# Three modulation products of the second layer leave the first layer's mixers

## The chip, the core and the metric

The kernel runs on one core of a Trainium2 chip. The metric is the time in microseconds (us) that the device needs for one execution; the time of the kernel before is the median of three runs. The core has a matrix engine (PE, with its weight loads as PEld), a vector engine (DVE), a scalar engine (ACT), a general engine (POOL) and a queue engine (SP) that does nothing here but issue transfers. ACT can issue transfers too. Each engine runs its own instructions in the order in which they stand in the program; semaphores hold an instruction back until what it needs is there.

## The reference, cut to what matters

Two layers of a network run over 1024 latent tokens and 256 context tokens of width 1024, all in f32:

```
for l in range(2):
    need_ctx = l < 1
    mod_l = split(silu(c)     @ ada_w[l] + ada_b[l], 6)     # latent rows
    mod_c = split(silu(c_ctx) @ ada_w[l] + ada_b[l], 6)     # context rows
    h  = rmsnorm(x, norm1_w[l])   * (1 + mod_l[1]) + mod_l[0]
    hc = rmsnorm(ctx, norm1_w[l]) * (1 + mod_c[1]) + mod_c[0]
    y, yc = four mixers (RG-LRU, HGRN2, SSD, MLA attention) of h @ w_in[l], hc @ w_in[l]
    x = x + mod_l[2] * (y @ w_out[l])
    h = rmsnorm(x, norm2_w[l]) * (1 + mod_l[4]) + mod_l[3]
    x = x + mod_l[5] * expert_choice_ffn(h, ...)            # 16 experts
    if need_ctx: the same for ctx with yc and mod_c
```

`ada_w[l]` is 1024 x 6144. Its six blocks of 1024 columns are needed at different times: blocks 0 and 1 by the first norm of a layer, block 2 behind the mixers, blocks 3 to 5 by the second norm and the experts. They depend on `c` and `c_ctx` alone, so each can be computed at any time ahead of its use.

## The kernel before

A layer runs as a set of threads (Python generators): `norm1` (first norm and the transposes of its 10 tiles of 128 tokens), the projections by `w_in` (`v` among them: 24 matmuls 128x256 a tile, evicted by ACT and written to memory from ACT's queue), the four mixers, `prep` and `mla` (attention: each prepared tile of queries and keys goes through memory and is read back by L1343), `lw` (loads of `w_out`), `wout` (the output projection, second norm and the router's logits), `route` (the choice of tokens for each expert), `woutc` and `routec` (the same for the context) and `exp` (the 16 experts). `Model.weave` steps the threads in turn by a table of priorities (`ORDER`; the lower the number, the earlier a thread is stepped) and by an account of when each engine comes free, and so fixes the order of the instructions on each engine. A thread stops at `wait(...)` until the named marks are in `self.done`, and at `room(n, "W")` until n tiles of the kind are free. Weights lie in tiles of 512 KB, tag `W`, of which there are 7.

`ada(l, i)` computes modulation blocks 2i and 2i+1 of layer l. It takes 8 steps; in each, two transfers on SP's queue bring 512 KB each of `ada_w` into `W` tiles (L405), and four f32 matmuls of 32x512 (`sT`, the activated `c` and `c_ctx`, against them) add to one accumulator, in four column groups of the array. In the trace one such matmul is two records, so a step is 8. Behind the 8 steps DVE adds the bias and ACT's queue writes the two rows to memory (L419). Product (0, 0) has its own thread at the kernel's start. The other five, (0, 1), (0, 2), (1, 0), (1, 1) and (1, 2), stand one behind another in the thread `ada` of layer 0, whose priority 20 puts its steps where the mixers leave room.

All transfers of SP's and ACT's queues share eight semaphores in turn, and a transfer that gets a semaphore waits until the one that had it before has landed. So a long run of transfers on one queue can hold up the other queue's.

Of the kernel before, what the change touches and what calls it, by code (L numbers as in the profile page):

```python
# [29 lines left out]
ORDER = [  # L30
    dict(derived=0.5, ada0=-2, ada=20, norm=-3, eproj=6.624, lru0=6.01, lru1=8.078, gate0=8.48, gate1=7.01, ssd=4.653,
         z=8.49, g=7, v=1.85, hgrn0=6.614, hgrn1=0.99, group0=1.91, group1=4.161, hout0=4.306, hout1=1.492, chunk=3.42,
# [8 lines left out]
    dict(derived=0.5, ada0=-2, ada=20, norm=-3, eproj=1, lru0=6.01, lru1=8.078, gate0=3.4, gate1=7.01, ssd=3.43, z=6.95,  # L41
         g=7, v=0.079, hgrn0=6.614, hgrn1=6.757, group0=1.91, group1=3.41, hout0=6.767, hout1=3.44, chunk=6.713, prep=1.5,
# [123 lines left out]
class Model:  # L166
# [210 lines left out]

    def ada(self, l, i, first=False):

# [15 lines left out]
        for k in range(8):  # L395
            if first:
                ws = [W[k // 2][:, k % 2, 0:1024], W[k // 2][:, k % 2, 1024:2048]]
                yield 2.5
            else:
                yield from self.room(2, "W")  # L400
                ws = []
                for hf in range(2):
                    w = self.t("W", [128, 1024])
                    c0 = 2048 * i + 1024 * hf
                    nc.sync.dma_start(w, wk[k][:, c0:c0 + 1024])  # L405
                    ws.append(w)
                yield 5.0
# [10 lines left out]
        for s in range(0 if first else 2):  # L418
            nc.scalar.dma_start(self.mod[l, s, 2048 * i:2048 * i + 2048].rearrange("(g n) -> g n", g=4),  # L419
                                mr.rearrange("(g r) n -> r g n", r=32)[s])  # L420
        if i == 0:
            self.done.add(f"mod{l}")
# [1097 lines left out]
    def wout(self, l, s, base, h2d, logits):  # L1520

        nc, a = self.nc, self.a
        c0, nt = (0, 2) if s else (2, 8)
        yield from self.wait(f"w{l}.0", *([f"woutc{l}.1"] if l == 0 and not s else []))
        yield from self.room(4)
# [526 lines left out]
    def layer(self, l):  # L2052
        need = l == 0
        self.yT = self.d([1024, NT])
        if l == 0:
            self.spawn(l, "derived", self.derived())
            self.spawn(l, "ada0", self.ada(0, 0, True))
            self.spawn(l, "ada", chain(self.wait("n0.9"), *[self.ada(*x) for x in ((0, 1), (0, 2), (1, 0), (1, 1), (1, 2))]))
        self.left[l] = 18
# [76 lines left out]
```

## Time and profile before

| | us |
|---|---|
| median of three runs | 2833.26 (2833.19 to 2836.4) |
| the profiled execution, its own time | 2837.1 |
| its span in the trace | 2835.3 |
| PE busy | 2421.0 (85%) |
| DVE busy | 1830.6 (65%) |
| ACT busy | 1183.7 (42%) |
| POOL busy | 908.6 (32%) |

The profile's times count from the start of the span. Layer 0 takes the first 1578 us (mixers up to some 920, output projection to 1088, routing to 1131, experts to 1572), layer 1 the rest. Busy shares are means over stages with different limits, so that what counts is the stage from which work is taken, and the stages to which it goes: in layer 0 the attention's start and what follows (611 to 735), the routing (1088 to 1131), and in layer 1 the first norm and the projections (1578 to 1710).

### The profile page before, as it was taken

The numbers are of one execution on the slowest core, as the hardware profiler recorded it, in microseconds if no ns is written. First come the engines' busy times: TensorE is split into PE (matmuls) and PEld (weight loads), VectorE is DVE, ScalarE is ACT, GpSimd is POOL, SyncE is SP. The second block draws the span as 40 slices with busy tenths as digits, with TensorE's granted clock in tenths as the row PEclk, the third lists the DMA queues.
The fourth block names the chain that finished last, engine by engine and source line by source line (L and its number), as shares of the span: only waits on it lengthen the run. The fifth ranks groups of instructions, "written<-read, shape, count | busy, mean of one in ns | idle before, by whom it ended". The sixth has DMA issues, their size and how long they took to land. (4 is left out here: it accounts for less than half of the span.)

```text
span 2835.3 us, 49820 instructions
## 1 busy us (share of the span) xinstructions
PE 2421.0 (85%) x19212; PEld 1850.4 (65%) x19212; DVE 1830.6 (65%) x3606; ACT 1183.7 (42%) x2010; POOL 908.6 (32%) x930
## 2 busy tenths in 40 slices
PE   5879999988898794889899599889968988669998
PEld 3758888544555572767677587779745556447786
DVE  5345476566786546676677746672787764578886
ACT  3345223234344222555455352422352342246675
POOL 3112232242531113233343522421353311324443
PEclk8889999999999896999999799989988999879999
DMA  6222135468212434688788511132331023559997
GB/s 250 63 67 65 58 92 184 134 218 288 82 51 97 158 116 136 235 263 282 264 280 283 160 49 42 55 98 80 115 113 49 23 95 131 199 187 377 376 366 244
DMA packets 243436, 455.40 MB, mean 161 GB/s; under 512 B 25688, under 2 KB 155096, under 8 KB 242176
## 3 DMA queue, kind: packets, MB, share of 16 engines
q1 hardware_dynamic: 190176, 365.75, 37.1%
q0 software_dynamic: 12096, 37.75, 5.6%
q10 hardware_dynamic: 40928, 48.72, 4.9%
q8 instruction: 151, 2.47, 0.4%
q14 instruction: 85, 0.70, 0.1%
HBM read 377.55 MB, written 74.60 MB: 159 GB/s over the span
## 5 line engine op out<-in xcount | busy, mean ns | idle before, releaser
L162 PE MATMUL ps<-A,W 128*128 128x512 f32 (+3 forms) x4160 | 972.2, 381 | 34.4 <-ACT W L162 31.5
L162 PEld LDWEIGHTS ps<-A,W 128*128 128x128 f32 x4160 | 742.4, 196 | 180.1 <-ACT W L162 35.3
L162 DVE TENSOR_TENSOR A<-C,A 128x1024 fp32r<-128x1024 f32 x310 | 406.8, 1342 | 129.8 <-ACT A L162 123.9
L162 ACT ACTIVATE M<-ps 128x512 f32<-128x512 f32 (+6 forms) x576 | 262.4, 468 | 533.1 <-PE ps L162 448.8
L162 ACT ACTIVATE A<-C 128x1024 fp32r<-128x1024 f32 x384 | 394.6, 1059 | 180.0 <-DMA C<-in_moe_w_down_dram 76.6
L162 POOL TENSOR_TENSOR A<-C,A 128x1024 fp32r<-128x1024 f32 x74 | 206.2, 2789 | 319.6 <-ACT A L162 303.8
L162 PE MATMUL ps<-W,A 128*128 128x256 f32 x1344 | 191.7, 299 | 6.6 <-DVE A L162 6.3
L162 PE MATMUL ps<-A,M 128*128 128x512 f32 x768 | 182.9, 393 | 2.1 <-ACT M L162 1.4
L162 PEld LDWEIGHTS ps<-W,A 128*128 128x128 f32 x1344 | 176.4, 202 | 9.4 <-DVE A L162 7.0
L162 POOL TENSOR_TENSOR C<-C,M 128x512 f32<-128x512 f32 x76 | 110.1, 1459 | 190.4 <-ACT M L162 129.4
L162 PEld LDWEIGHTS ps<-A,M 128*128 128x128 f32 x768 | 142.4, 188 | 36.4 <-DVE M L162 3.0
L162 PE MATMUL ps<-cf,M 128*128 128x128 f32 (+3 forms) x416 | 75.0, 309 | 98.8 <-DVE M L162 63.9
L162 DVE TENSOR_TENSOR C<-C,M 128x512 f32<-128x512 f32 (+2 forms) x196 | 128.8, 669 | 40.7 <-ACT M L162 39.3
L162 PE MATMUL ps<-C,A 128*32 128x128 f32 (+1 forms) x2528 | 145.3, 285 | 0.0
L162 PEld LDWEIGHTS ps<-C,A 128*32 128x32 f32 (+1 forms) x2528 | 132.9, 125 | 11.3 <-issue 6.4
L162 PE MATMUL ps<-A 96*128 96x512 f32 (+3 forms) x368 | 132.3, 415 | 9.3 <-ACT A L162 4.0
L162 PEld LDWEIGHTS ps<-cf,M 128*128 128x128 f32 (+2 forms) x416 | 55.7, 157 | 128.7 <-issue 43.6
L162 PE MATMUL ps<-M,M 128*128 128x64 f32 (+4 forms) x720 | 90.4, 284 | 56.4 <-DVE M L162 46.1
L162 PE MATMUL ps<-A,C 128*128 128x512 f32 x352 | 134.0, 411 | 1.5 <-DVE C L162 1.4
L162 ACT ACTIVATE W<-ps 128x512 fp32r<-128x512 f32 (+2 forms) x156 | 65.9, 476 | 163.1 <-PE ps L162 162.7
L162 ACT ACTIVATE C<-ps 128x512 f32<-128x512 f32 (+4 forms) x116 | 53.8, 469 | 183.1 <-PE ps L162 170.0
L162 POOL TENSOR_TENSOR W<-W,C 128x512 f32<-128x512 f32 x33 | 49.7, 1524 | 249.4 <-DVE W L162 184.1
(244 smaller groups left out, 3838.0 us busy)
## 6 DMA issues: line engine op xcount, KB each, us to landing
C<-in_moe_w_gate_dram SPq DMA_DIRECT2D x128, 512.0 KB
C<-in_moe_w_up_dram SPq DMA_DIRECT2D x128, 512.0 KB
C<-in_moe_w_down_dram SPq DMA_DIRECT2D x128, 512.0 KB
W<-in_ada_w_dram SPq DMA_DIRECT2D x80, 512.0 KB
W<-in_w_in_dram SPq DMA_DIRECT2D x40, 512.0 KB
C<-dr SPq DMA_DIRECT2D x29, 512.0 KB
dr<-M ACTq DMA_DIRECT2D x114, 128.0 KB
M<-dr SPq DMA_DIRECT2D x46, 256.0 KB
```

Source lines behind the costliest of these rows:

```text
L162: return f(*args, **kw)
```

## The change

Product (1, 0), which the first norm of layer 1 needs, gets a thread of its own, `ada1`, with priority 32. It starts when tile 7 of layer 0's `wout` is done, that is in the routing, with its 16 loads on SP's queue. Products (1, 1) and (1, 2) move into layer 1, as its thread `ada` with priority 20; their 32 loads are issued on ACT's queue (`later=True`). `wout` now waits for the marks of its layer's products 1 and 2 as well. (0, 1) and (0, 2) stay where they were. The number of matmuls is the same.

```diff
-    dict(derived=0.5, ada0=-2, ada=20, norm=-3, eproj=6.624, ...
+    dict(derived=0.5, ada0=-2, ada=20, ada1=32, norm=-3, eproj=6.624, ...
...
-    def ada(self, l, i, first=False):
+    def ada(self, l, i, first=False, later=False):
...
-                    nc.sync.dma_start(w, wk[k][:, c0:c0 + 1024])
+                    (nc.scalar if later else nc.sync).dma_start(w, wk[k][:, c0:c0 + 1024])
...
+        self.done.add(f"ada{l}.{i}")
         if i == 0:
             self.done.add(f"mod{l}")
...
-        yield from self.wait(f"w{l}.0", *([f"woutc{l}.1"] if l == 0 and not s else []))
+        yield from self.wait(f"ada{l}.1", f"ada{l}.2", f"w{l}.0", *([f"woutc{l}.1"] if l == 0 and not s else []))
...
-            self.spawn(l, "ada", chain(self.wait("n0.9"), *[self.ada(*x) for x in ((0, 1), (0, 2), (1, 0), (1, 1), (1, 2))]))
+            self.spawn(l, "ada", chain(self.wait("n0.9"), *[self.ada(*x) for x in ((0, 1), (0, 2))]))
+            self.spawn(l, "ada1", chain(self.wait("wout0.7"), self.ada(1, 0)))
+        else:
+            self.spawn(l, "ada", chain(*[self.ada(1, i, later=True) for i in (1, 2)]))
```

Three places show what stands in an engine's row. In the rows, `W` tiles from `in_ada_w_dram` and matmuls with `sT` are the products'; `DMA M<-dr ... 128x384` is a query or key tile read back (L1343, in the kernel after the change L1344). The line numbers after the change are one higher from L420 on.

SP's queue in layer 0, where the attention reads its tiles back, before:

```order
L1343 DMA M_10192<-dr_8413 128x384
L384 DMA M_10210<-in_ada_b_dram 32x512 x4
L405 DMA W_10216<-in_ada_w_dram 128x1024
L405 DMA W_10218<-in_ada_w_dram 128x1024
L1343 DMA M_10228<-dr_8413 128x384
L1343 DMA M_10267<-dr_8413 128x384
L1343 DMA M_10286<-dr_8413 128x384
L1343 DMA M_10305<-dr_8413 128x384
L1343 DMA M_10324<-dr_8413 128x384
L405 DMA W_10345<-in_ada_w_dram 128x1024
L405 DMA W_10347<-in_ada_w_dram 128x1024
L1343 DMA M_10357<-dr_8413 128x384
```

and after:

```order
L1344 DMA M_10414<-dr_8458 128x384
L1344 DMA M_10433<-dr_8458 128x384
L1344 DMA M_10458<-dr_8458 128x384
L856 DMA M_11006<-dr_9830 128x2x256
L856 DMA M_11007<-dr_151 128x2x256
```

The read-backs now follow one another with no load of `ada_w` between them, and what follows the last is SSD's next reads (L855 before).

PE's queue at the start of layer 1, from the last experts' matmuls (`C,M`) over the tiles' transposes (`cf,C`) to the first projection (`W,A`), before:

```order
L162 MATMUL ps_19287<-C_19155,M_19255 32x256 x4
L162 MATMUL ps_19427<-cf_66,C_19322 128x128 x4
L162 MATMUL ps_19428<-cf_66,C_19322 128x128 x4
L162 MATMUL ps_19441<-cf_66,C_19324 128x128 x4
L162 MATMUL ps_19442<-cf_66,C_19324 128x128 x4
L162 MATMUL ps_19474<-cf_66,C_19391 128x128 x4
L162 MATMUL ps_19475<-cf_66,C_19391 128x128 x4
L162 MATMUL ps_19493<-W_19331,A_19423 128x256
```

and after:

```order
L162 MATMUL ps_19106<-C_18974,M_19074 32x256 x4
L162 MATMUL ps_19193<-W_19194,sT_68 32x512 x2
L162 MATMUL ps_19193<-W_19196,sT_68 32x512 x2
L162 MATMUL ps_19193<-W_19233,sT_68 32x512 x2
L162 MATMUL ps_19193<-W_19235,sT_68 32x512 x2
L162 MATMUL ps_19309<-cf_66,C_19141 128x128 x4
L162 MATMUL ps_19193<-W_19438,sT_68 32x512
L162 MATMUL ps_19310<-cf_66,C_19141 128x128 x4
L162 MATMUL ps_19323<-cf_66,C_19143 128x128 x4
L162 MATMUL ps_19324<-cf_66,C_19143 128x128 x4
L162 MATMUL ps_19193<-W_19438,sT_68 32x512
L162 MATMUL ps_19193<-W_19440,sT_68 32x512 x2
```

13 of the two products' 64 matmuls now stand ahead of the first projection's; the other 51 are cut into 20 runs among the projections' matmuls that follow.

ACT's queue at the first tiles of `v` (`M<-ps 128x256` is the eviction of a tile of `v`, `A<-ps 128x4x128` a copy of a tile's transposes), before:

```order
L162 ACTIVATE M_19519<-ps_19493 128x256
L162 ACTIVATE C_19320,s_2505_19798<-C_19579 128x1024
L928 DMA dr_19328<-M_19519 128x2x128
L162 ACTIVATE A_19423<-ps_19540 128x4x128
L162 ACTIVATE A_19424<-ps_19541 128x4x128
L162 ACTIVATE M_19608<-ps_19582 128x256
```

and after:

```order
L162 ACTIVATE M_19401<-ps_19375 128x256
L405 DMA W_19522<-in_ada_w_dram 128x1024
L929 DMA dr_19147<-M_19401 128x2x128
L405 DMA W_19650<-in_ada_w_dram 128x1024
L162 ACTIVATE M_19610<-ps_19584 128x256
L162 ACTIVATE A_19305<-ps_19542 128x4x128
L162 ACTIVATE A_19306<-ps_19543 128x4x128
```

Loads of the products now stand between an eviction and the copies behind it.

## Rows read from the trace of the kernel before

**Rows 1.** The page: busy us, share of the span, instructions of each engine.

```profile
PE 2421.0 (85%) x19212; PEld 1850.4 (65%) x19212; DVE 1830.6 (65%) x3606; ACT 1183.7 (42%) x2010; POOL 908.6 (32%) x930
```

**Rows 2.** Windows in layer 0, all instructions; columns as in the first line.

```profile
core 0: us, PE busy (x) PEld busy (x) DVE busy (x) ACT busy (x) POOL busy (x), PEclk, DMA share, GB/s
611.00:631.00 20.00, 14.63 (x77) 4.47 (x75) 15.79 (x53) 6.89 (x15) 12.39 (x20) 1.00 0.83 282
631.00:662.00 31.00, 21.80 (x103) 9.69 (x104) 10.43 (x28) 8.59 (x24) 1.94 (x2) 0.78 0.91 310
662.00:735.00 73.00, 68.19 (x431) 37.66 (x430) 57.56 (x137) 33.25 (x92) 35.55 (x63) 1.00 0.62 212
```

**Rows 3.** The same windows, the instructions on tile sT alone.

```profile
611.00:631.00 20.00, 8.91 (x40) 1.39 (x40) 0.00 (x0) 0.00 (x0) 1.00 0.83 282
631.00:662.00 31.00, 10.79 (x34) 1.30 (x34) 0.00 (x0) 0.00 (x0) 0.78 0.91 310
662.00:735.00 73.00, 17.76 (x94) 2.63 (x94) 0.00 (x0) 0.00 (x0) 1.00 0.62 212
```

**Rows 4.** Timeline of SP's queue, layer 0: start, us, instruction, count.

```profile
629.26 0.38 SPq L1343 DMA_DIRECT2D M<-dr  x1
...
639.63 5.65 SPq L384 DMA_DIRECT2D M<-in_ada_b_dram  x4
...
656.75 6.14 SPq L1343 DMA_DIRECT2D M<-dr  x6
```

**Rows 5.** Timeline of SP's queue, the same place in layer 1.

```profile
2094.88 0.35 SPq L1343 DMA_DIRECT2D M<-dr  x1
...
2098.89 15.16 SPq L1343 DMA_DIRECT2D M<-dr  x17
```

**Rows 6.** PE's waits from 611 to 662: total us, times, longest.

```profile
PE ps L162 <- DMA W<-in_ada_w_dram: 9.0, 8, 3.3
PE ps L162 <- DMA M<-dr: 4.3, 2, 3.8
```

**Rows 7.** Timeline of PE, layer 0 (in brackets the idle time before, and what ended it).

```profile
616.80 1.05 PE L162 MATMUL ps<-W,sT 128*32 128x512 f32 x4 [0.57 <-DMA W<-in_ada_w_dram]
...
620.02 1.13 PE L162 MATMUL ps<-M,W 128*128 128x512 f32 x2
...
712.79 1.05 PE L162 MATMUL ps<-W,sT 128*32 128x512 f32 x2
713.76 1.91 PE L162 MATMUL ps<-C,C 64*128 64x128 f32 x12
...
908.96 1.22 PE L162 MATMUL ps<-A,W 128*128 128x512 f32 x2 [7.53 <-ACT W L162]
```

**Rows 8.** Timeline of PE in the routing of layer 0.

```profile
1098.14 1.96 PE L162 MATMUL ps<-cf,A 128*128 128x128 f32 x8 [3.21 <-DMA A<-dr,ic]
1112.87 0.56 PE L162 MATMUL ps<-cf,M 32*128 32x32 f32 x2 [12.77 <-DVE M L162]
```

**Rows 9.** Windows at the start of layer 1, all instructions; columns as in rows 2.

```profile
1580.00:1590.00 10.00, 0.00 (x0) 0.00 (x0) 4.56 (x16) 5.06 (x9) 0.77 (x1) 0.50 0.99 371
...
1600.00:1610.00 10.00, 6.59 (x32) 6.20 (x33) 9.93 (x10) 3.65 (x8) 8.77 (x12) 0.53 0.40 113
1610.00:1630.00 20.00, 18.50 (x155) 18.03 (x155) 19.31 (x38) 9.22 (x18) 13.04 (x9) 1.00 0.12 34
1630.00:1700.00 70.00, 70.00 (x393) 60.27 (x392) 32.14 (x36) 39.85 (x52) 16.60 (x18) 1.00 0.18 50
```

**Rows 10.** Timeline of PE at the start of layer 1.

```profile
1590.93 1.12 PE L162 MATMUL ps<-cf,C 128*128 128x128 f32 x4 [19.24 <-POOL C L162]
...
1605.29 4.94 PE L162 MATMUL ps<-W,A 128*128 128x256 f32 x24
...
1627.88 3.14 PE L162 MATMUL ps<-W,A 128*128 128x256 f32 x24 [1.50 <-DVE A L162]
...
1703.14 1.56 PE L162 MATMUL ps<-A,W 128*128 128x256 f32 x9 [0.61 <-ACT W L162]
1707.56 24.95 PE L162 MATMUL ps<-A,W 128*128 128x256 f32 x144 [2.87 <-DVE W L162]
```

More of the change, by code (lines that the diff above doesn't have):

```diff
@@ L30 @@
 ORDER = [
-    dict(derived=0.5, ada0=-2, ada=20, norm=-3, eproj=6.624, lru0=6.01, lru1=8.078, gate0=8.48, gate1=7.01, ssd=4.653,
+    dict(derived=0.5, ada0=-2, ada=20, ada1=32, norm=-3, eproj=6.624, lru0=6.01, lru1=8.078, gate0=8.48, gate1=7.01, ssd=4.653,
          z=8.49, g=7, v=1.85, hgrn0=6.614, hgrn1=0.99, group0=1.91, group1=4.161, hout0=4.306, hout1=1.492, chunk=3.42,
@@ L40 @@
          "ada0:ada+20": 5.7, "ada:ada+29": 5}),
-    dict(derived=0.5, ada0=-2, ada=20, norm=-3, eproj=1, lru0=6.01, lru1=8.078, gate0=3.4, gate1=7.01, ssd=3.43, z=6.95,
+    dict(derived=0.5, ada0=-2, ada=20, ada1=32, norm=-3, eproj=1, lru0=6.01, lru1=8.078, gate0=3.4, gate1=7.01, ssd=3.43, z=6.95,
          g=7, v=0.079, hgrn0=6.614, hgrn1=6.757, group0=1.91, group1=3.41, hout0=6.767, hout1=3.44, chunk=6.713, prep=1.5,
```

## The prediction, made before the changed kernel was run

> **What bounds the kernel now.** The page first: PE is busy 85% of the span, the next engine 65% [rows 1], so PE's time is the first thing to count. But the work that moves sits in a few stages, and in each the bound is another. So the second reading is windows: one row for each stage, all instructions, and beside it the same window with the products' instructions alone. The third is the timeline of the queue or engine that waits there, to see what a waiting instruction waits for. Three stages lose or gain work.
>
> Layer 0, 611 to 735 us, loses it. From 611 to 631 DVE is busy 15.8 of 20 us and the products take 8.9 us of PE [rows 2, 3]. From 631 to 662 nothing is full but the transfers: DVE 10.4 of 31, ACT 8.6, POOL 1.9, PE 21.8 of which 10.8 are the products' own, while the DMA engines are busy 0.91 of the time at 310 GB/s [rows 2, 3]. That is a stage that waits for loads, and PE's waits name them: 9.0 us in 8 waits on the products' loads, 4.3 on the attention's read-backs [rows 6]. From 662 to 735 PE is busy 68.2 of 73 us, 17.8 of them products, with DVE behind it at 57.6 [rows 2, 3].
>
> The routing of layer 0 (1088 to 1131) and the start of layer 1 (1578 to 1740) get it. In the routing PE waits 12.77 us in one piece for a DVE chain [rows 8]. At the start of layer 1 the DMA engines are full (0.99 at 371 GB/s), PE does nothing until 1590.93, then DVE binds (9.9 of 10 us, then 19.3 of 20), and from 1630 to 1700 PE is full to the last microsecond [rows 9, 10].
>
> **What is removed (a gain).** 24 steps: 192 records, of which rows 3 hold 168. Four terms.
>
> First, the read-backs. In layer 0 they take SP's queue from 629.26 to 656.75 + 6.14 = 662.89, 33.6 us for 20 transfers, with the products' loads and a bias load of 5.65 us among them [rows 4]. In layer 1, with no products, they go from 2094.88 to 2098.89 + 15.16 = 2114.05, 19.2 us for 18 [rows 5], 21.3 for 20. Their new order has no product's load among them. Gain 33.6 - 21.3 = 12.3 us. Ends: 16 if layer 0 then needs no more than its PE work without the products asks for, 7 if only the bias load and little else falls out.
>
> Second, the last tiles of `prep`. At 620.02 a matmul of the key projection starts that stood behind two product runs, each of which waited for its load; the first of them began at 616.80, so it is late by up to 620.02 - 616.80 = 3.2 us [rows 7]; I take 3.1. Ends 0 and 5.
>
> Third, 662 to 735. A run of products costs about 0.97 us whatever it holds: the one of two records at 712.79 lets the next matmul start at 713.76 [rows 7]. The runs here come to 17.8 us [rows 3]. Without them PE has 68.2 - 17.8 = 50.4 us of work and DVE 57.6 [rows 2, 3], so DVE is what would be late next, and the gain can't exceed 73 - 57.6 = 15.4. DVE does not get to 100% in such a stretch; at 0.90 the stage lasts 64, which gives 9. I take 9.5; ends 3 and 15.
>
> Fourth, the last three steps (899 to 918): behind one run PE idles 7.53 us anyway [rows 7], so only the last counts, with half of its 1 us: 0.5.
>
> Sum: 12.3 + 3.1 + 9.5 + 0.5 = **25.4 us less**, ends about 15 and 32. Time gained at 735 is carried on, since all threads of the layer move up together.
>
> **Product (1, 0) in the routing (a cost).** Its 16 loads join the first expert weights' on SP's queue, and its 8 steps are 8 to 9 us of PE. PE's idle pieces there (12.77, 3.21 and others [rows 8]) hide nearly all. What is not hidden is where a run stands ahead of a short matmul of the routing's chain of PE and DVE (the counts, the slots): two or three runs of about 1 us, and the last step among the first expert's matmuls. **+2**, ends 0 and 7 (a load that lands late ahead of such a matmul: 3.3, the longest such wait of rows 6).
>
> **Products (1, 1) and (1, 2) in layer 1 (a cost).** Five parts.
>
> The start: the first tiles' loads share full DMA engines [rows 9] with three or four of the products' loads. At 371 GB/s 512 KB take 1.4 us; two of them ahead of the tiles', and with them the shared semaphores, are +3. Ends 0 and 6.
>
> Here the Trainium skill (DMA: Bandwidth & Descriptors, Issuing engines are not separate DMA queues) speaks against the change: transfers from SP and ACT run on the same 16 DMA engines, and a second issuing engine saves issue time only. By that rule all four loads would stand in the tiles' way, 5.6 us in place of 3, and the sum below would be 2.6 higher; the 0.99 of rows 9 agrees that no bandwidth is left there.
>
> PE: 13 matmuls stand ahead of the first projection, where PE idles 19.24 us and more [rows 10]: nothing. The other 51 make 20 runs, at 0.97 us each 19.4 us, all in PE's full stretch. That is the price of the cut: two products in whole steps would have 16 runs.
>
> What of it is absorbed: the idle pieces of 1.50 us at 1627.88, 0.61 at 1703.14 and 2.87 at 1707.56 [rows 10], -5. And until 1610 PE runs at a granted clock of 0.53, close to the lower of its two levels (1.2 GHz; from 1610 it is 1.00, the upper, 2.4 GHz), in the projection of 4.94 us at 1605.29 [rows 9, 10]; before it PE had idled for most of 25 us. The products' runs fill part of that, and if the upper level is granted earlier for it, up to half of the group is saved: -2.4. Ends -2.4 and 0.
>
> ACT: each load waits for its tile, which the matmuls of a load some three earlier free, and the evictions and copies of `v` are queued behind it. A load issued behind an eviction has about one tile's time until its run. I count +2 for runs that wait; ends 0 and 9 (the 9.0 us of rows 6, the nearest case).
>
> Sum: 3 + 19.4 - 5 - 2.4 + 2 = **+17**, ends 6 and 30. Below, DVE's full stretch up to 1630 would hide the nine or ten runs that stand there; above, no idle is recovered.
>
> **The sum.** -25.4 + 2 + 17 = -6.4. On the profiled execution: 2837.1 - 6.4 = 2830.7. That execution lies 3.8 above the median of 2833.26, and 1.8 of it is outside its span; the difference is carried to the median: **2827**.
>
> **The rivals.**
>
> *Slower: ACT's queue holds up `v`.* Each load on ACT waits for a run on PE, the run waits for the load, and the copies of a tile's transposes wait behind both. For: the new order puts loads between an eviction and the copies behind it, and only three of seven `W` tiles are left while `v` holds four. Against: ACT is busy 9.2 of 20 us there [rows 9], so that there is slack. Price: 9 us of waits in place of 2, no absorption of 5 and no clock's gain of 2.4: cost 3 + 19.4 + 9 = 31, sum -25.4 + 2 + 31 = +8: 2841. It decides from the point at which these waits pass 2 + 6.4, the net gain.
>
> *No change: the steps were filler.* The runs from 662 to 735 filled PE's time while DVE's chain set the pace; then the third term is 3 or less. For: DVE at 57.6 of 73 [rows 2]. Against: PE idles only 4.8 of 73 us, which is not how a stage looks that waits for DVE. Sum -18.9 + 2 + 17 = 0: 2833.
>
> *Much faster: the projections hide them.* From 1590 to 1630 DVE is as full as PE [rows 9], and if it sets the pace the runs there, about half of the 20, cost nothing. Cost 17 - 9 = 8, sum -15: 2818. Against: PE's 18.5 of 20 us leave 1.5 us.
>
> That the change does not do what it says would show as read-backs in layer 0 that still take 33 us; the new order excludes it.
>
> **How the numbers follow.** A measurement of this kernel tells apart 0.2%, 5.7 us. The forecast gets 0.38 (its own range 2821 to 2832), slower 0.26, no change 0.20, much faster 0.16. The forecast lies only just beyond the 0.2% line: of its chance 0.27 falls below 2827.6 and 0.11 within. Much faster counts whole as faster, with 0.03 of no change: 0.46. Slower by over 0.2% is the slower rival but for 0.02, and 0.02 of no change: 0.26. The rest, 0.28, is within. The range takes in both outer cases with their ends: 2811 to 2844.
>
> **What would show it.** In the profile after: read-backs of layer 0 within some 21 us, and no PE wait on `in_ada_w_dram` there; the stretch behind it of about 64 us in place of 73; the first experts' matmul at the same distance from the logits as before, or 2 us more; the first transposes of layer 1 some 3 us later against the last expert, and 20 product runs up to 1740 with few waits in front of them. I am wrong if the stretch behind the read-backs keeps its 73 us, or if PE's waits on product loads in layer 1 come to over 8 us.

## The result, and the profile after

The kernel after the change takes 2864.88 us (median of four runs, 2859.8 to 2873.3) against 2834.21 for the kernel before on the same chip (2833.19 to 2836.4): a ratio of 1.0111, 95% interval 1.0089 to 1.0134. It is slower by 1.1%, 31 us, where 6 us less were forecast, and lies outside the range of 2811 to 2844. The profiled execution took 2859.8, the lowest of its four, 22.7 above the profiled one of before (2837.1). A later session gave 1.0108 [1.0081, 1.0136] for the same kernel.

The first place to look is the page. Of after, its span and shares (compare [rows 1]):

```profile
span 2857.3 us, 49815 instructions
PE 2444.5 (86%) x19212; PEld 1861.5 (65%) x19212; DVE 1832.8 (64%) x3606; ACT 1182.2 (41%) x2009; POOL 912.9 (32%) x930
```

PE is busy 23.5 us longer (2421.0 before) with the same number of matmuls. So PE's own work has become slower, by its clock or by the finer cut of the products; PE does not only wait more. To see where, I matched each matmul of after with its counterpart in before and took the difference of their start times. Negative is earlier than before:

```
at before's us   where                                  after - before, us
   590           ahead of the read-backs                      -5.3
   665           read-backs done                             -20.9
   745                                                       -17.6
  1072           output projection                           -17.6
  1150           first experts (routing done)                -14.6
  1550           last experts                                -17.9
  1591           first transposes of layer 1                 -11.1
  1605           first matmul of v                           -11.4
  1643           end of v                                     +1.2
  1716           projections                                 +21
  2823           end                                         +20.7
```

Code that the change does not touch shifts by some 5 us from one execution to the next, as at 590, so that no step of less than that is read from this table alone. Three things stand out: 15 us gained by 665, none behind it, and 39 us lost from the last experts to 1716. Behind 1716 nothing changes any more.

**The gain, layer 0.** The SP queue's timeline of after, where the attention reads its tiles back (start, duration, line, what is moved, count):

```profile
624.80 0.87 SPq L1344 DMA_DIRECT2D M<-dr  x2
626.48 0.32 SPq L1299 DMA_DIRECT2D dr<-M  x1
626.90 13.14 SPq L1344 DMA_DIRECT2D M<-dr  x18
```

The twenty take 15.2 us (624.80 to 626.90 + 13.14 = 640.04), where [rows 4] showed 33.6. The matched stretch from 635 to 662 takes 14.9 us in place of 27.5: -12.6. From 611 to 635 it is -2.5. Now the stretch behind, which before ran from 662 to 735 [rows 2, 3], as a window of after over the same matmuls (us, then busy time and number of instructions of PE, PEld, DVE, ACT, POOL, the granted clock, the share of DMA, GB/s):

```profile
642.10:716.50 74.40, 62.83 (x333) 43.23 (x332) 54.72 (x133) 24.19 (x63) 26.01 (x35) 0.81 0.13 41
```

It has lost 17.8 us of product runs and is 1.4 us *longer*. Before, PE's other work took 68.2 - 17.8 = 50.4 us at a granted clock of 1.00; now the same work takes 62.8 at 0.81. What PE waits for there (total, times, longest):

```profile
PE ps L162 <- DVE M L162: 5.6, 3, 3.2
PE ps L162 <- DVE nm L162: 4.4, 3, 2.2
```

So DVE's chain leaves PE small gaps, which the products had filled. And the clock swings in this stretch, where in before it stays at 1.00 (three pieces of the same stretch of after):

```profile
651.00:657.00 6.00, 6.00 (x28) 4.28 (x27) 2.81 (x12) 3.35 (x8) 0.00 (x0) 0.50 0.00 0
658.00:688.00 30.00, 24.75 (x154) 14.95 (x151) 24.75 (x62) 10.00 (x26) 9.87 (x15) 1.00 0.19 58
689.00:705.00 16.00, 15.79 (x56) 12.45 (x57) 10.34 (x21) 1.39 (x4) 7.05 (x11) 0.50 0.01 2
```

In the pieces at 0.50 PE is full, so that there its own pace counts and not DVE's.

**The routing.** It lasts 45.9 us in place of 42.9 (+2.9; +5.1 in the later execution). PE's wait of [rows 8] now holds runs of product (1, 0), the first of them behind a wait for its load:

```profile
1085.60 6.18 PE L162 MATMUL ps<-W,sT 128*32 128x512 f32 x20 [5.74 <-DMA W<-in_ada_w_dram]
1121.64 1.06 PE L162 MATMUL ps<-W,sT 128*32 128x512 f32 x8
```

**The loss, the start of layer 1.** Windows of after over the matmuls that stood from 1605 to 1643 and from 1643 to 1718 (before: 36.5 us of PE in 38, 71.5 in 75):

```profile
1593.60:1644.20 50.60, 48.26 (x345) 36.99 (x344) 30.27 (x53) 15.96 (x33) 21.36 (x23) 0.98 0.54 168
1644.20:1739.10 94.90, 86.29 (x419) 64.51 (x418) 35.27 (x37) 40.92 (x52) 14.19 (x15) 0.93 0.32 99
```

and in the same windows the products' instructions alone (PE, PEld, DVE, ACT, clock, DMA, GB/s):

```profile
1593.60:1644.20 50.60, 12.05 (x54) 1.75 (x54) 0.00 (x0) 0.00 (x0) 0.98 0.54 168
1644.20:1739.10 94.90, 10.14 (x48) 1.38 (x48) 0.00 (x0) 0.00 (x0) 0.93 0.32 99
```

The two stages are 12.6 and 19.8 us longer; with the late first transposes (-17.9 to -11.1) that is 39 us. PE's waits from 1555 to 1740:

```profile
PE ps L162 <- DMA W<-in_ada_w_dram: 25.3, 7, 9.4
PE ps L162 <- ACT W L162: 6.7, 2, 4.3
PE ps L162 <- DVE W L162: 1.9, 1, 1.9
```

25.3 us on the products' loads are far over the 8 that the prediction named as its own disproof. But most of them lie ahead of the first projection (1593.9), where PE in before waited for the normed tiles (from 1572 to 1605):

```profile
PE ps L162 <- POOL C L162: 27.8, 4, 19.2
```

In the two windows themselves (1593.6 to 1739.1) PE's waits in after are:

```profile
PE ps L162 <- ACT W L162: 6.7, 2, 4.3
PE ps L162 <- DMA W<-in_ada_w_dram: 2.3, 3, 1.6
PE ps L162 <- DVE W L162: 1.9, 1, 1.9
```

PE's timeline shows where the long ones stand (start, duration, operation, count, and in brackets the idle time ahead and its releaser); `cf,C` are a tile's transposes, `W,A` is `v`:

```profile
1563.21 3.36 PE L162 MATMUL ps<-W,sT 128*32 128x512 f32 x8 [9.45 <-DMA W<-in_ada_w_dram]
...
1577.97 1.92 PE L162 MATMUL ps<-W,sT 128*32 128x512 f32 x4 [8.67 <-DMA W<-in_ada_w_dram]
1579.83 1.12 PE L162 MATMUL ps<-cf,C 128*128 128x128 f32 x4
...
1590.43 1.92 PE L162 MATMUL ps<-W,sT 128*32 128x512 f32 x2 [4.02 <-DMA W<-in_ada_w_dram]
1592.28 1.97 PE L162 MATMUL ps<-cf,C 128*128 128x128 f32 x8
1593.90 2.34 PE L162 MATMUL ps<-W,A 128*128 128x256 f32 x10
```

The first tile's transposes stand directly behind a run that waited for its load. That load is the one at 1570.22 on ACT's queue, behind a tile's square that itself waited 17.95 us for the tile:

```profile
1566.78 1.06 ACT L162 ACTIVATE C<-C 128x1024 f32<-128x1024 f32 x1 [17.95 <-DMA C<-dr]
1567.74 0.19 ACT L162 ACTIVATION_READ_ACCUMULATOR C<-C 128x1 f32 x1
1570.22 0.33 ACTq L405 DMA_DIRECT2D W<-in_ada_w_dram  x1
```

That run is only the last part of the late start. The first tile's load and the end of its norm on POOL, in after:

```profile
1560.10 0.83 SPq L444 DMA_DIRECT2D C<-dr  x2
1576.59 1.65 POOL L162 TENSOR_TENSOR C<-C,M 128x512 f32<-128x512 f32 x1 [19.71 <-DVE C L162]
```

and load, square and norm in before:

```profile
1578.22 0.79 SPq L443 DMA_DIRECT2D C<-dr  x2
1581.86 1.06 ACT L162 ACTIVATE C<-C 128x1024 f32<-128x1024 f32 x1 [11.88 <-DMA C<-dr]
1589.23 1.65 POOL L162 TENSOR_TENSOR C<-C,M 128x512 f32<-128x512 f32 x1 [10.70 <-DVE C L162]
```

From the issue of the load to the square it is 6.7 us where it was 3.6, from the square to the end of the norm 11.5 where it was 9.0, and from there to the transposes 1.6 where they followed at once. Of the 6.8 us by which the transposes are late (-17.9 to -11.1), about 3.0 are the tile's load, 2.4 the chain behind it, and 1.5 the run on PE.

And on SP's queue, which issues none of these loads, the projections' weights fall behind. Its timeline of after:

```profile
1578.88 7.01 SPq L444 DMA_DIRECT2D C<-dr  x5
1612.09 3.27 SPq L646 DMA_DIRECT2D W<-in_lru_w_r_dram  x4
...
1644.03 75.37 SPq L530 DMA_DIRECT2D W<-in_w_in_dram  x6
```

and its longest wait there:

```profile
SPq L646 <- DMA W<-in_ada_w_dram: 22.1, 1, 22.1
```

SP stands 22.1 us behind a landing of a product's load, and the first of these projection weights (L530) is issued at 1644.03, where before it was at 1603.20; the second is 2.7 us later than before and the third 22.6. The 6.7 us in which PE waits for `ACT W` are the part of it that shows in PE's waits: ACT's copies of those weights, which wait for their landing.

### The profile page after: what moved, and what is told of

It is laid out like the page before. It is cut to its first block, busy times and chain, and to the rows that moved or that the text cites. A ratio compares the mean times of both kernels' runs of the same rounds, so it can differ in the third digit from the quotient of the medians.

```text
span 2857.3 us, 49815 instructions
## 1 busy us (share of the span) xinstructions
PE 2444.5 (86%) x19212; PEld 1861.5 (65%) x19212; DVE 1832.8 (64%) x3606; ACT 1182.2 (41%) x2009; POOL 912.9 (32%) x930
## 5 line engine op out<-in xcount | busy, mean ns | idle before, releaser
L162 PE MATMUL ps<-A 96*128 96x512 f32 (+3 forms) x368 | 136.0, 426 | 15.7 <-ACT A L162 6.5
L162 POOL TENSOR_TENSOR W<-W,C 128x512 f32<-128x512 f32 x33 | 50.3, 1543 | 247.5 <-DVE W L162 188.2
```

The lines of the kernel that those rows point to most:

```text
L162: return f(*args, **kw)
```

## The experiments

Unless told otherwise an edit is made to the kernel after; the kernel before ran on the same chip each time. "Stage" is the move of the matched matmuls from the last experts (1550) to the projections (1716 or later): 39 us in after.

**One product, or two.** Only (1, 0) leaves layer 0 (`e1_only10`):

```diff
-            ... *[self.ada(*x) for x in ((0, 1), (0, 2))]))
+            ... *[self.ada(*x) for x in ((0, 1), (0, 2), (1, 1), (1, 2))]))
...
-        else:
-            self.spawn(l, "ada", chain(*[self.ada(1, i, later=True) for i in (1, 2)]))
```

> One part alone: product (1, 0) moves into the routing, products (1, 1) and (1, 2) stay in layer 0's thread behind (0, 2). Theory (the loss sits in layer 1's first stage, 39 us by the two traces, and the routing costs 3 at most): layer 1 is as before, the read-backs keep their product loads, so 2832 to 2838, within 0.2% of the kernel before. Rival (the new product in the routing is what costs, by way of the first experts' weights): 2845 or more.

Measured 2842.39 us, 1.0022 [1.0009, 1.0034]. Between the read-backs loads still stand (635 to 662: -2.5 us), and the routing is 5.1 us longer. The other half, (1, 0) stays and two products move into layer 1 (`e2_only_l1`):

```diff
-            ... *[self.ada(*x) for x in ((0, 1), (0, 2))]))
-            self.spawn(l, "ada1", chain(self.wait("wout0.7"), self.ada(1, 0)))
+            ... *[self.ada(*x) for x in ((0, 1), (0, 2), (1, 0))]))
```

> The other part alone: (1, 0) stays in layer 0's mixers, (1, 1) and (1, 2) move to layer 1 on ACT's queue. Theory: the start of layer 1 costs the same 39 us as in the changed kernel and the read-backs gain some 6 to 12 us, so 2858 to 2868. Rival (the routing's product is what costs): 2822 to 2830.

Measured 2866.79, 1.0097 [1.0076, 1.0118], with a stage of 39 us and 25.2 us of waits on product loads. The loss belongs to the two products in layer 1.

**Is it ACT's queue?** The same loads on SP's queue (`e3_sp`):

```diff
-            self.spawn(l, "ada", chain(*[self.ada(1, i, later=True) for i in (1, 2)]))
+            self.spawn(l, "ada", chain(*[self.ada(1, i) for i in (1, 2)]))
```

> The changed kernel with the loads of (1, 1) and (1, 2) on SP's queue in place of ACT's. Theory A (the runs on PE and the three W tiles that v leaves set the cost, whichever queue issues): 2852 to 2866, PE still waits 20 us or more on the products' loads around the start of layer 1. Theory B (ACT's queue is the cause: loads wait behind evictions, evictions behind loads): the cost of the stage falls from 39 to about 20, 2838 to 2848.

Measured 2881.59, 1.0156 [1.0139, 1.0174]: the stage costs 52 us. PE's waits from 1540 to 1760:

```profile
PE ps L162 <- DMA W<-in_ada_w_dram: 28.7, 4, 16.2
PE ps L162 <- POOL C L162: 14.6, 4, 6.2
```

The waits on the loads are not those of a queue that ACT's evictions hold up: they stay when ACT issues none, and now the tiles are late too (`POOL C`, the normed tile). So ACT's queue is not needed for the loss. Nor does PE wait from 1555 to 1740 of after for ACT's copies of transposes (`ACT A`), by which the slower rival of the prediction has ACT's queue hold up `v`: it had the sign, and this part of its mechanism does not show. What part ACT's queue has in after's 39 us this run can't tell, since on SP's queue the loads hold up other transfers.

**Runs or loads?** All 32 loads stay, the runs shrink to 8 of 512 columns (`e4_tiny`, which leaves out the rest of the two products):

```diff
+                n = 8 if later else 512
-                nc.tensor.matmul(pm[32 * g:32 * g + 32, :], ..., ws[g // 2][:, 512 * (g % 2):512 * (g % 2) + 512],
+                nc.tensor.matmul(pm[32 * g:32 * g + 32, 0:n], ..., ws[g // 2][:, 512 * (g % 2):512 * (g % 2) + n],
...
```

> The changed kernel with the matmuls of products (1, 1) and (1, 2) cut to 8 of 512 columns (the rest of these two products is left out, the modulation rows get the bias alone there), all 32 loads kept: what the loads cost without the runs on PE. Theory (of the 39 us of layer 1's start some 20 are PE runs of about 1 us, the rest waits for loads, for converted projection weights and the late start): the stage costs 15 to 22, so 2836 to 2846. Rival (the loads' waits are only there because PE's runs delay what frees the W tiles): under 10, so 2828 or less. Rival (PE's runs are filler, the loads are all of it): 30 or more, 2852 and up.

Measured 2865.57, 1.0094 [1.0069, 1.0118], against 1.0111 with full runs: the stage still costs 39 to 41 us. The products' instructions in it, and PE's waits from 1563 to 1760:

```profile
1599.00:1760.00 161.00, 4.86 (x96) 3.03 (x96) 0.00 (x0) 0.00 (x0) 0.91 0.38 111
```

```profile
PE ps L162 <- DMA W<-in_ada_w_dram: 37.1, 12, 9.9
PE ps L162 <- ACT W L162: 8.1, 2, 5.4
```

This is the run that decides against the prediction's main term. 22.2 us of runs have become 4.9, and the stage is as long. Where the saving went is read from the two windows, over the same matmuls as above:

```profile
1599.20:1654.00 54.80, 42.38 (x350) 39.41 (x349) 28.85 (x54) 14.90 (x31) 22.43 (x20) 0.87 0.57 165
1654.00:1744.00 90.00, 77.47 (x406) 64.20 (x406) 34.63 (x38) 40.70 (x52) 14.18 (x15) 0.92 0.30 91
```

PE idles 24.9 us in them, where after has 10.9, and its other work takes 115.0 in place of 112.4, at a lower clock. Of the idle time 7.1 us are waits on the products' loads, 8.1 on `ACT W`; the other 30.0 us of the 37.1 lie ahead of the windows. So the price is not that of the runs: it comes with the loads, in part by waits for them and in part by what they hold up. The small runs and small loads of 64 KB together, with an order that differs a little (`e8_small`; the matmuls read the first 8 columns of a tile):

```diff
+                    m = 128 if later else 1024
-                    (nc.scalar if later else nc.sync).dma_start(w, wk[k][:, c0:c0 + 1024])
+                    (nc.scalar if later else nc.sync).dma_start(w[:, 0:m], wk[k][:, c0:c0 + m])
...
```

> As the kernel with matmuls of 8 columns, and each of the 32 loads cut from 512 to 64 KB (the first 128 of 1024 columns; the same part of the two products is left out). Neither the runs nor the bytes are left, only the trips: issue, tile, landing. Theory (the trips set the pace: a load of 64 KB takes nearly as long from issue to landing as one of 512, and the evictions stand behind it): 20 or more for the stage, 2842 and up. Rival (the bytes: full DMA engines beside the norm's loads, long landings): under 10, 2833 or less.

Measured 2859.75, 1.0087 [1.0061, 1.0113]; the stage costs 22 to 26 us. PE's waits from 1540 to 1780:

```profile
PE ps L162 <- DMA W<-in_ada_w_dram: 32.4, 15, 7.9
```

With an eighth of the bytes and hardly any runs, over half of the loss is left. What is left comes with the trips: a free tile, a turn on the queue, a landing, and what they hold up. 26.8 of the 32.4 us lie before 1600; behind that PE waits longest for `ACT W` (8.6 us). No run takes these apart. One product in place of two ((1, 2) left out, `e9_one`):

```diff
-        for k in range(8):
+        for k in range(0 if later and i == 2 else 8):
...
```

> The changed kernel with product (1, 2) left out (its modulation rows get the bias alone), (1, 1) as it is: 16 loads and 32 matmuls in layer 1 in place of 32 and 64. Theory (the loads' pace sets the cost: each has to wait for a W tile that an earlier run frees, so that the cost goes with their number, and the late start of some 7 us stays): the stage costs 18 to 25 in place of 39, 2840 to 2850. Rival (the first loads, beside the tiles' own, are all of it and the rest is hidden): 30 or more, 2855 and up.

Measured 2845.27, 1.0035 [1.0017, 1.0053]; the stage costs 14.5 us, so the second product costs more (25) than the first. Runs kept and loads taken away instead (28 of the 32, the first two tiles serving all steps, `e5_noload`):

```diff
+                if not later or k == 0:
                     yield from self.room(2, "W")
...
-            if not first:
+            if not first and (not later or k == 7):
```

> The changed kernel with 28 of the 32 loads of (1, 1) and (1, 2) left out: each product multiplies all 8 steps with the two W tiles of its first step (wrong products there), the runs on PE kept: what the runs cost without the loads. Theory: 18 to 24 us for the stage, 2838 to 2846, PE's waits on the products' loads at layer 1's start under 5 after the first. Rival (the loads' waits are all of it): under 8, 2828 or less.

Measured 2870.2, 1.0102 [1.0072, 1.0132]. This edit holds two of the seven `W` tiles throughout, and the order in layer 1 parts from that of after; the projections then wait for tiles. Only up to the end of `v` can it be read: some 7 us where after has 19, and there 64 of the 80 records of the runs stand ahead of the first projection, where after has 26. Taken whole it decides nothing.

**Is it the number of `W` tiles?** An eighth tile (and one `M` less), in before (`e11_before_w8`) and in after (`e12_after_w8`):

```diff
-        self.bufs = {"A": 4, "C": 10, "W": 7, "M": 14, "s1": 6}
+        self.bufs = {"A": 4, "C": 10, "W": 8, "M": 13, "s1": 6}
```

> The kernel before with 8 W tiles in place of 7 and 13 M tiles in place of 14 (one more weight tile fits in no other way): the control for the next. 2826 to 2846, since the order changes a little with it.

> The changed kernel with 8 W tiles and 13 M tiles. Beside v's four tiles the products' loads now have four in place of three, and the order of the second product moves back behind v. Theory (the supply of tiles, by which each load waits for an earlier run, sets the pace): the first product's part up to the end of v costs less than the 19 us of the changed kernel (-17.9 at the last expert to +1.2 at the end of v), some 10 to 14; the whole, with the second product later, 10 to 30 over its control. Rival (supply is no matter; the runs that PE's order puts ahead of the transposes are): the same 19 us up to the end of v.

Before with it: 2913.4, 1.0274 [1.0237, 1.0312]; after with it: 2896.77, 1.0215 [1.0184, 1.0245]. Between the two the change now gains 17 us, and the stage costs 21. But the order differs everywhere, and the second product falls much later in it. It agrees with a shortage of tiles and does not prove one.

**Other places.** The two products held until `v` is done (`e10_late`):

```diff
-            self.spawn(l, "ada", chain(*[self.ada(1, i, later=True) for i in (1, 2)]))
+            self.spawn(l, "ada", chain(self.wait("v1"), *[self.ada(1, i, later=True) for i in (1, 2)]))
```

> The changed kernel with the two products of layer 1 held back until v is done, so that none of their loads stands beside the norm's and v's four W tiles are free again. Theory (what costs is the scarce W tiles and the queue of evictions during v, and the late start): no late start, PE's waits on product loads under 8 us, PE's runs paid in part: 10 to 22 for the stage and what follows, 2832 to 2845. Rival (PE is full from 1630 on, so that every run and every projection weight that comes late for want of a tile is paid): 30 or more, 2852 and up.

Measured 2890.34, 1.0196 [1.016, 1.0233]: worse. SP's queue between 1600 and 1900 waits with the projections' weights (L530) for tiles that matmuls have to free (in before such waits come to 116.3 us in 7 from 1600 to 1850):

```profile
SPq L530 <- PE ps L162: 153.0, 8, 34.5
```

All three products in layer 0, behind the read-backs (`e6_behind`, whose edit is shown), and then the same with (1, 0) in the routing (`e7_split`):

```diff
-            ... *[self.ada(*x) for x in ((0, 1), (0, 2))]))
+            ... *[self.ada(*x) for x in ((0, 1), (0, 2))], self.wait("qk0.9.1"), *[self.ada(*x) for x in ((1, 0), (1, 1), (1, 2))]))
-            self.spawn(l, "ada1", chain(self.wait("wout0.7"), self.ada(1, 0)))
-        else:
-            self.spawn(l, "ada", chain(*[self.ada(1, i, later=True) for i in (1, 2)]))
```

> A third place: all three products stay in layer 0, in the same thread behind (0, 1) and (0, 2), but wait for the mark of the last query or key tile read back, so that they stand behind the read-backs; layer 1 and the routing are as before. Theory (the read-backs' stage is worth 12 to 15 us and the product runs of 662 to 735 were filler that hid behind DVE): 2820 to 2828, faster than both. Rival (the runs pushed on to 662 to 920 are paid there in full, some 20 us more): 2838 or more.

> As the one before with (1, 0) in the routing, where the change put it, and (1, 1) and (1, 2) behind the read-backs. Theory: 0 to 5 us worse than with all three behind the read-backs if those are filler there: 2821 to 2831. Rival (runs behind the read-backs are paid): better than it by up to 8.

2850.67, 1.0051 [1.003, 1.0073], and 2846.62, 1.0031 [1.0014, 1.0047]. In the first, matmuls are 20 us early at 677 and only 6.9 at 743 (the stretch from 662 to 735 takes 80.1 us), and 920 to 1088, which now holds 15.7 us of product runs, is longer by 15.8: there they are paid in full.

**What is the gain worth alone?** The three products left out, their rows written from the bias at the start of layer 1 (`e13_none`):

```diff
-        for k in range(8):
+        for k in range(0 if later else 8):
...
-            self.spawn(l, "ada1", chain(self.wait("wout0.7"), self.ada(1, 0)))
...
-            self.spawn(l, "ada", chain(*[self.ada(1, i, later=True) for i in (1, 2)]))
+            self.spawn(l, "ada", chain(*[self.ada(1, i, later=True) for i in (0, 1, 2)]))
```

> The changed kernel with products (1, 0), (1, 1) and (1, 2) left out wherever they stood (no loads, no matmuls; the modulation rows of layer 1 get the bias alone): what taking the 24 steps out of layer 0's mixers is worth when nothing has to be paid for them elsewhere. Theory (12 to 18 us by the traces so far, the read-backs' share, and nothing or a loss behind them): 2818 to 2825. Rival (the prediction's 25 us): 2808 to 2813.

2838.5, 1.001 [0.9994, 1.0025]: a kernel with 96 fewer matmul instructions and 48 fewer loads is no faster. At the last experts it is 12.3 us ahead of before, at layer 1's first transposes 1.6 behind, since the norm now waits for rows written just ahead of it. With (1, 0)'s rows moved to the routing, where after has that product (`e14_none2`):

```diff
-        for k in range(8):
+        for k in range(0 if l else 8):
...
```

> The changed kernel with products (1, 0), (1, 1) and (1, 2) left out again, but with the bias rows of (1, 0) written where the change puts that product, in the routing, so that the first norm of layer 1 doesn't wait for them as it did in the kernel that wrote all three at the start of layer 1. Theory (removing the 24 steps is worth 12 to 17 us up to the end of layer 0 and no more): 2818 to 2825. Rival (even this is lost again, because what DVE has left behind the read-backs catches up with the gain): within 5 us of the kernel before.

2839.08, 1.0008 [0.9991, 1.0025]. Ahead by 14.3 at 674 and 4.9 at 1550, behind by 2.9 at the first transposes: the eight bias loads of the other two stand among the norm's own on SP's queue:

```profile
1577.27 4.30 SPq L384 DMA_DIRECT2D M<-in_ada_b_dram  x4
1582.31 2.15 SPq L447 DMA_DIRECT2D C<-dr  x2
1584.56 7.57 SPq L469 DMA_DIRECT2D M<-dr  x8
```

With them ran the kernel after once more, unedited (`e15_again`):

> The changed kernel once more, beside the one without the products on the same chip: what the three products cost in the places where the change puts them. Theory: 2860 to 2873, 38 to 48 us over the kernel without them, nearly all of it between the last expert of layer 0 and the end of layer 1's projections. Rival (part of the loss has to do with the order of layer 1, not with the products): under 30 us over it.

2866.85, 1.0108 [1.0081, 1.0136], stage 38 to 40 us, and 28 us over the kernel without the products. That is the rival's number: in the kernel without them the same stage costs some 8 us too (4.9 ahead at 1550, 3.5 behind at 1716), by its bias loads, so that some 30 of the 38 to 40 are the products'. All rows in the routing (`e16_none3`, with the shortened loop of the last):

```diff
-            self.spawn(l, "ada1", chain(self.wait("wout0.7"), self.ada(1, 0)))
-        else:
-            self.spawn(l, "ada", chain(*[self.ada(1, i, later=True) for i in (1, 2)]))
+            self.spawn(l, "ada1", chain(self.wait("wout0.7"), *[self.ada(1, i) for i in range(3)]))
```

> Products (1, 0), (1, 1) and (1, 2) left out, and the bias rows of all three read and written in layer 0's routing, so that nothing at all of them stands at the start of layer 1 (in the kernel before this one eight bias loads stood among the norm's loads there and the first transposes came 8 us later). Theory (the steps taken out of layer 0 are worth some 8 to 14 us at the last expert and layer 1 keeps them): 2822 to 2828. Rival (the gain is eaten in layer 0's experts, whose weight loads set their pace): within 3 us of the kernel before. The prediction's 25 us would give 2810.

2841.91, 1.0033 [1.0018, 1.0048]. Ahead by 14.5 at 705; the routing, which now holds the row writes and bias loads, then takes 8.8 us more. In all three the stretch behind the read-backs is 2.7 to 3.1 us longer than before, at a clock of 0.81 to 0.82. Each of the three loses some 8 to 14 us at a place where the rows of its own edit are written or read (13.9, 7.8 and 8.8), so that they show what these kernels gain, and not what the steps alone are worth.

**The clock alone.** To the last kernel I added the products' matmuls, in their old place in layer 0, on a constant tile and with no load (`e17_fill`):

```diff
+    def fill(self):
+        pm = self.p()
+        for k in range(8):
+            yield 5.0
+            for g in range(4):
+                nc.tensor.matmul(pm[32 * g:32 * g + 32, :], self.sT[:, k, :], self.cf[:, 0:512], start=k == 0, stop=k == 7)
+            yield "s"
...
+            ... *[self.ada(*x) for x in ((0, 1), (0, 2))], self.fill(), self.fill(), self.fill()))
```

> The kernel without the three products' loads (their rows hold the bias alone, written in the routing, as in the one before), but with their 96 matmuls kept in layer 0's thread, on a constant tile that needs no load. Theory (the product runs cost nothing from 662 to 735, because without them PE waits more, its granted clock falls from 1.00 to about 0.8 and the rest of its work there gets longer by what the runs took): the read-backs' gain of some 14 us stays, the clock of that stretch is back at 0.95 or more, and the stretch takes no more than the 75.8 us that it took without any product. Rival (the runs are paid like other PE work, and the stretch without them is bound by DVE alone): clock up too, but the stretch 5 to 15 us longer, 81 to 91.

2834.97, 1.0004 [0.9984, 1.0024]. The stretch as a window, first without the fill (`e16_none3`), then with it, then the fill's instructions alone:

```profile
649.90:725.60 75.70, 63.43 (x332) 44.15 (x331) 54.79 (x133) 24.02 (x63) 25.81 (x35) 0.81 0.13 40
```

```profile
648.90:727.10 78.20, 73.56 (x455) 42.10 (x454) 56.45 (x137) 24.97 (x64) 25.98 (x35) 0.91 0.14 43
```

```profile
648.90:727.10 78.20, 17.67 (x118) 2.93 (x118) 0.00 (x0) 0.00 (x0) 0.91 0.14 43
```

17.7 us of added matmuls lengthen it by 2.5 us. PE's other work falls from 63.4 to 73.56 - 17.67 = 55.9 us, and the clock rises from 0.81 to 0.91. Other work times clock is 50.4 in before, 50.9 in after, 51.4 and 50.9 here: the same work, slowed by the clock alone. The clock did not come back to 1.00, and the 78.2 us lie between the two expectations. The whole kernel, with more work, stands 0.3% better against before than the one without (the intervals overlap a little, and part of it comes from another stretch, 2101 to 2210, whose clock fell to 0.81 in the one and not in the other).

The other kernels with this order bear the clock out and limit the gain. Over the same matmuls, other work times clock lies between 50.3 and 52.0 in all seventeen. In the twelve without a product run in the stretch (`e2_only_l1` among them) it lasts 74.0 to 78.4 us at 0.76 to 0.83. With some 17 us of runs it lasts 73.0 in before, 78.2 in `e17_fill`, 80.1 in `e6_behind` and 81.6 in `e7_split`, at 0.90 to 1.00. Against the mean of the twelve, 76 us, such runs cost from nothing to some 5 us there, far less than their own time; that they shorten the stretch is seen in before alone.

None of these kernels beats the kernel before.

## Why the prediction was wrong

It was wrong in two steps, and both failed by the same thing: a stage was costed on PE's busy time as the trace of before had it.

**Layer 1: forecast +17, measured +39.** Term by term, from the windows above (before: 108.0 us of PE in 113):

| term | forecast | measured in after |
|---|---|---|
| late start | 3 | 6.8 |
| product runs | 19.4 | 22.2 |
| PE's other work (clock) | -2.4 | 134.56 - 22.20 - 108.02 = +4.3 |
| idle, absorbed or added | -5 + 2 | 10.9 - 5.0 = +6 |

The price of the runs was near. The failed step is "what of it is absorbed": the idle pieces of before were not used, they grew, since the runs came with loads. And a row-by-row repair of the table would still mislead, because the terms don't add: with hardly any runs (`e4_tiny`) the stage costs as much, and without most of the bytes too (`e8_small`) it costs over half. The term that was missing is the time that the 32 loads take to pass through tiles and queues which `v` and the projections want as well, and what that does to the loads behind them (SP's 22.1 us, the first projection weight 41 us later). The prediction counted only PE's waits on the loads themselves, +2 with an end of 9.0 [rows 6]. Where PE is full that was right, 2.3 us; what it left out is the waits behind them, `ACT W` with 6.7 us, and the loads ahead of the first tile.

The late start had the right place and too small a size. The page's rule that I set beside it (the Trainium skill, DMA: Bandwidth & Descriptors, Issuing engines are not separate DMA queues) gave 5.6; measured were 6.8. That it is nearer than my 3 is luck: both price the shared bandwidth, and the tile's own load came 3.0 us late, as I had it. The rest is the chain behind the load (2.4) and a run on PE that waits for the load issued at 1570.22, behind ACT's square (1.5), and neither was in the sum. And which queue issues was worth 13 us (39 on ACT, 52 on SP), with PE waiting 14.6 us for normed tiles in the second; that this is by what stands behind the loads in the queue is likely and not shown.

**Layer 0: forecast -25.4, measured some -14 behind the stretch.**

- Read-backs, -12.3: measured -12.6 in after, -12.1 and -12.5 in `e16_none3` and `e17_fill`. The place and the size were right, the size in part by luck: the queue takes 15.2 us and not the 21.3 of [rows 5], so it is 18.4 us shorter, of which PE gains 12.6.
- The last tiles of `prep`, -3.1: measured -2.5. Right.
- The stretch behind, -9.5 with an end of -3: measured +1.4, and +1.0 to +5.4 in the eleven other kernels without product runs there. Wrong in sign, and this is the failed step of layer 0. The step "68.2 - 17.8 = 50.4 us of work" takes 50.4 as a constant, but it was measured at a clock of 1.00, which the runs themselves had held up. At 0.81 the same work is 62.8, more than DVE's 57.6.
- The last steps, -0.5: too small to see.

There is an account of this that I had not weighed. The Trainium skill (TensorE: Matmul & The Clock Gate, A second HAM failure mode: psum-queue depth-cycling) tells of a kernel whose PE idles briefly between groups of matmuls so often that its clock swings between the two levels. The trace agrees: 10 us of short waits on DVE in 74, pieces at 0.50 and at 1.00 (1.2 and 2.4 GHz) by turns, and a mean of 0.81. The prediction used the clock only for the place that receives the runs, and not for the one that loses them.

The "no change: the steps were filler" rival had this part right for another reason. It held that DVE sets the pace; in fact PE is slower, and DVE's gaps make it so. It was given 0.20 and needed layer 1 at +17. The slower rival (0.26) put layer 1 at +31, nearest to the 39, and shared the -25.4 of layer 0.

**Routing: forecast +2 (0 to 7), measured +2.9 and +5.1.** Within its ends.

**The sum.** -15.1 by 662, +1.4 in the stretch, +2.9 and +39 make +28, on a profile that was 5.3 early before anything had changed: +23, where the profiled execution is 22.7 longer. Between the stages that the change touches, identical stretches differ by up to 4.5 us in either direction and nearly cancel.

Open: why the runs of one kernel spread over 3 us in one session and 25 in another (the kernel before: 2833.19 to 2836.4, and 2824.6 to 2849.94 beside `e17_fill`); how the 39 us divide between tiles, semaphores and landing times, since `e5_noload` and the pair with eight tiles were both spoiled by a changed order; and the clock between 2101 and 2210, 0.81 to 0.92 in kernels whose work there is the same.

## What to carry to other kernels

Work that stands as filler in another stage's gaps may cost far less than its own time, so before moving it, ask what clock the work around it has *because* of it, and cost that work at the lower clock. For the place that receives it, count the trips of its loads through the buffers that the stage needs for itself, not its matmuls, and try a version with the matmuls shrunk and the loads kept: it tells at once which of the two sets the price. And a kernel that leaves the moved work out altogether bounds the gain cheaply, if what the edit itself adds is small; here none of three was faster than before.

## What the runs showed of the hardware

PE's busy time for one and the same work went as the inverse of the granted clock: 50.4 us at 1.00, 55.9 at 0.91, 62.8 and 63.4 at 0.81, and so in thirteen more kernels (time times clock 50.3 to 52.0). The stretch from 2101 to 2210 of layer 1 shows it again: 90.2 us at 0.92 in `e15_again`, 92.8 at 0.89 in before, 100.4 at 0.81 in `e16_none3`. Matmuls that fill gaps of one to three microseconds gave back most of their own time by it: 17.7 us of them cost 2.5 between `e16_none3` and `e17_fill`. And a queue that issues none of a stream of loads can stand behind it: SP waited 22.1 us for the landing of a load that ACT had issued.
